# First-phase attention heads straight from PSUM behind the key units, and one 512-token range for group 0's output projection and first norm

## The chip, the cores and the metric

The kernel runs on one core of one Trainium2 chip. The metric is device time in microseconds, from one launch, and lower is better. In the tables, PE is TensorE (matmuls), PEld its weight loads, DVE VectorE, ACT ScalarE, POOL GpSimd, and SP the SyncE engine, whose queue issues nearly all DMA.

## The reference

One layer of a hybrid encoder runs over two groups of tokens with the same weights: 1024 tokens of a new stream ("prompt") and 32 tokens of a running stream with a cache of 256 ("sample"). All arithmetic is float32.

```python
mod = silu(c) @ w_ada + b_ada                       # six vectors of 1024 per stream
h = x * (1 + sc1) + sh1
mq, mk, mv, mo, mi, mf, fq, fk, fv, ff, gu, gv = split(h @ w_in)
hm = head_norm(mlstm(mq, mk/8, mv, mi, mf)) * g * sigmoid(mo)   # 4 heads of 64, chunked recurrence
hf = softmax(fq fk^T / 8 + F_t - F_s, causal) @ fv              # 8 heads of 64, F = cumsum(log_sigmoid(ff))
hg = gu * (tril(ws) @ layer_norm(gv) + bs)                      # 4 groups, blocks of 128 tokens
mix = concat(hm, hf, hg) @ w_o
x = layer_norm(ALPHA * x + (1 + g1) * mix)
y = (silu(h2 @ w_gate) * (h2 @ w_up)) @ w_down      # h2 = x * (1 + sc2) + sh2, width 2816
x = layer_norm(ALPHA * x + (1 + g2) * y)
```

The outputs are x and the states: the attention's keys, values and log forget values, and the mLSTM's matrices.

## The kernel before

**Layout and precision.** Activations lie transposed, features on the 128 partitions and tokens along the free axis, in 8 tiles of 128 features. The 1056 tokens are cut into group 0 (tokens 0 to 511) and group 1 (512 to 1055, the sample in its last 32). A float32 product is made from three passes in TensorE's fast float32 type: each operand is split into a high part and a remainder, and `gemm` (L111) adds hi x hi, hi x lo and lo x hi, at lines L117, L118 and L119. `weights` (L94) loads 512 KB into one of three "raw" buffers (L87 is the load in `load`), makes the high part on ScalarE (L105) and the remainder on VectorE or POOL (L106). A matmul writes into a PSUM bank of 512 columns; the pool "g" has three.

**Ranges.** `MM` cuts each group into two ranges, (0, 256) and (256, 512) for group 0 and two of 272 for group 1. `WIDE` is the single range (0, 512).

**Order.** The code is traced in program order. The Tile framework then fixes each engine's instruction order ahead of the run, from priorities (program order) and its own model of the timing. `tc.high_priority(n)` moves the traced instructions up by n places and `issue_after` puts them behind a given one. On the chip every engine runs its list strictly in order, SP's DMA list included.

**Stages around the change.** After the first units come the values and gates (`gates`: the cumulative sums and maxima of the forget values, long chains on VectorE over few partitions, that store the rows `dfs` which every attention head reads). Then follows the string `ORDER`, unit by unit: `q`h makes queries and keys of attention head h, `f`h attends for the head's first 512 queries, `k0 k1` make the mLSTM's keys (`k1p`: its weights' remainder on POOL), `s` prepares the mLSTM's states, `m`j is its chunk j, `v` and `o` are units with tokens on the partitions, `a` is one unit of `ada` (two loads of 512 KB, 16 matmuls, two transposes, a ScalarE copy and four small VectorE operations). `f` and `m` run at high priority.

A `q` unit before the change is `fm_unit` with `evac_qk` for each range: ScalarE makes the high part `qkh` (L366), VectorE the remainder `qkl` (L367), POOL their sum `qkr` (L368) for the key output; all three are stored (`dqh`, `dql`, `o_kT`). `fox` (L672) then loads nine pieces back into the tiles k1, k2, qp, q2 and v. The scores are L717 and L718, the softmax's exponential L726, the transposes L753, the products with the values L761 and L766.

After the phase come the gMLP units, the second-half tokens of heads 2 and 3, and group 0's output projection: `wo` is called once for each range of 256, so it loads the eight weight tiles of w_o twice. Each output tile passes `sublayer_end`: POOL subtracts the pivot (`less`, L977), VectorE adds the residual (L982), and `ln_sum` squares on ScalarE (L871) and adds up on POOL (L875) and VectorE (L877). `ln1` then takes the means through TensorE (L887), the reciprocal root (L894 to L898), and per tile a multiplication (L999), an addition (L1000), an affine on ScalarE (L1003) and the split into `hh` (L1007) and `hl` (L1008), the operands of the up projection. The four units of heads 4 to 7 for group 1's tokens follow, then `ln1_res` (the residual's affine, 16 operations on POOL, L1017), the second phase's attention and the feed-forward units `up` (SiLU at L1055 to L1059) and `down`. The ada units 20 to 23 come behind the first four up units.

Of the kernel before, what the change touches and what calls it, by code (L numbers as in the profile page):

```python
# [7 lines left out]
F32 = mybir.dt.float32  # L8
F32R = mybir.dt.float32r
# [6 lines left out]
P = 128  # L16
D = 1024
KT = 8
# [23 lines left out]
ORDER = "q0 f0 q1 a f1 a q2 f2 k0 k1p s a q3 f3 a v q4 f4 a q5 f5 o a m0 q6 f6 a m1 q7 m2 f7 a m3"  # L42
# [23 lines left out]
def f(ap):  # L66
    return ap.bitcast(F32)


class Kernel:  # L70
# [288 lines left out]
    def evac_qk(self, h):  # L359
        nc = self.nc  # L360

        def evac(o, n, ps):
            hi = self.t(self.sm, [P, 272], F32R, "qkh", 3)
            lo = self.t(self.sm, [P, 272], F32R, "qkl", 2)
            kr = self.t(self.sm, [P, 272], F32, "qkr", 3)
# [9 lines left out]

    def evac_mqk(self, i, scale):
        nc = self.nc

        def evac(o, n, ps):
            r = self.t(self.sm, [P, 272], F32, "qkr", 3)  # L380
# [291 lines left out]
    def fox(self, h, chunks):  # L672
# [4 lines left out]
        t = lambda shape, dt, tag, bufs: self.t(mx, shape, dt, tag, bufs)  # L677
        b = self.foxbufs
        k1 = t([P, nk], F32R, "k1", b[0])
        qp = t([P, nq], F32R, "qp", b[1])  # L680
        k2 = t([68, nk], F32R, "k2", b[2])
        q2 = t([68, nq], F32R, "q2", b[1])
        v = t([P, nb, P], F32R, "v", b[3])
        qs = slice(q0, q1)
        self.load(f(qp[0:64]), self.dqh[h, 0:64, qs])
        self.load(f(qp[64:128]), self.dql[h, 0:64, qs])
        self.load(f(k1[0:64]), self.dqh[h, 64:128, :nk])
        self.load(f(k1[64:128]), self.dqh[h, 64:128, :nk])
        self.load(f(q2[0:64]), self.dqh[h, 0:64, qs])
        self.load(f(q2[64:68]), self.dfs[h, 2:6, qs])  # L690
        self.load(f(k2[0:64]), self.dql[h, 64:128, :nk])
        self.load(f(k2[64:68]), self.dfs[h, 0:4, :nk])
        self.load(f(v), self.dv[:, :nb, h * P:(h + 1) * P])
# [5 lines left out]
    def fox_chunk(self, h, tiles, W, nq, k1, k2, qp, q2, v):  # L699
# [71 lines left out]
        tmp = t([64, nq], F32, "fo", 1)  # L771
        r = t([64, nq], F32, "fr", 1)
        nc.scalar.copy(tmp[:, :nq], o[64:128, :nq])
        nc.vector.tensor_tensor(r[:, :nq], o[0:64, :nq], tmp[:, :nq], ALU.add)
# [80 lines left out]

    def ln_pivot(self, st, z, sl):
# [7 lines left out]
    def ln_sum(self, st, z, m, sl):  # L864
# [5 lines left out]
        sq = self.t(self.p2, [P, 272], F32, "tmp", 4)[:, :sl.stop - sl.start]  # L870
# [29 lines left out]
    def ln_stats(self, st, sl):  # L900
# [3 lines left out]
        v = self.t(self.p2, [P, 272], F32, "tmp", 4)[:, :sl.stop - sl.start]  # L904
# [68 lines left out]
    def sublayer_end(self, c, z, m, ps, gate, st, a, b):  # L973
# [3 lines left out]
        less = lambda: self.nc.gpsimd.tensor_tensor(z[:, m, sl], z[:, m, sl], st["pv"][:, sl], ALU.subtract)  # L977
# [13 lines left out]
    def ln1(self, c, st, a, b):  # L991
# [3 lines left out]
        for k in range(KT):  # L995
# [4 lines left out]
            (nc.gpsimd if k % 4 == 1 else nc.vector).tensor_tensor(zk, zk, e, ALU.add)  # L1000
            h = self.t(self.p2, [P, 272], F32, "tmp", 4)[:, :b - a]
# [250 lines left out]
    def run(self):  # L1252
# [71 lines left out]
        self.foxbufs = (2, 1, 1, 2, 3)  # L1324

        def emit(x):
# [7 lines left out]
            if x[0] == "q":  # L1334
                self.fm_unit(w3[2 + i], self.evac_qk(i), (0, 1) if i < QD else (0,), eng)
# [63 lines left out]
        for g, (j0, nj) in enumerate(GROUPS):  # L1399
# [195 lines left out]
```

## Time and profile before

| | us |
|---|---|
| median of 3 runs | 1391.1 (1388.4 to 1398.72) |
| profiled execution | 1389.64 |
| its span, first to last instruction | 1387.8 |
| PE busy | 1344.1 (97%) |
| DVE busy | 1030.4 (74%) |
| ACT busy | 641.0 (46%) |
| POOL busy | 260.2 (19%) |

The mean granted TensorE clock is 0.990 of full speed. A row of a view of groups reads: line, engine, operation, tile written <- tiles read, shapes, count | busy us, mean ns of one | idle us of the engine just before them and what ended it. A row of waits reads: the waiting instruction <- what released it: us in total, times, longest. A row of the chain or of the timeline begins with its start in us.

### The profile page before, as it was taken

How to read it: one execution, taken by the hardware profiler on the slowest of the kernel's cores; microseconds unless marked ns; L12 is line 12 of the kernel's file. 1: busy time of each engine (PE TensorE's matmuls, PEld its weight loads, DVE VectorE, ACT ScalarE, POOL GpSimd, SP SyncE). 2: the span in 40 equal slices, each digit the busy share in tenths (PEclk: the TensorE clock that was granted, in tenths of full speed). 3: DMA queues.
4: the chain of work that ended last, by engine and by line, in shares of the span. 5: the costliest groups of instructions: out<-in, count | busy, mean ns of one | idle time of the engine just before them, and what ended most of it. 6: DMA issues, size and time to landing. Idle time of an engine off the chain costs nothing.

```text
span 1387.8 us, 25846 instructions
## 1 busy us (share of the span) xinstructions
PE 1344.1 (97%) x9651; PEld 1236.2 (89%) x9651; DVE 1030.4 (74%) x2190; ACT 641.0 (46%) x1249; POOL 260.2 (19%) x292
## 2 busy tenths in 40 slices
PE   7999999999999799999999999999999999999996
PEld 4899988899999678888887889899999999999996
DVE  5548656678788657777776766678898988888777
ACT  3313234444555344545544455345574544545355
POOL 0103200052267400000000000264610000000341
PEclk9999999999999899999999999999999999999998
DMA  9764577585765665554543442564587767453321
GB/s 361 260 217 135 165 239 213 173 252 167 234 209 152 194 182 155 141 140 118 138 117 86 112 122 81 192 176 132 159 221 200 217 163 205 145 176 113 102 90 65
DMA packets 133557, 233.09 MB, mean 168 GB/s; under 512 B 22308, under 2 KB 75180, under 8 KB 133432
## 3 DMA queue, kind: packets, MB, share of 16 engines
q1 hardware_dynamic: 128120, 221.34, 51.7%
q0 software_dynamic: 5168, 9.96, 4.7%
q8 instruction: 76, 1.25, 0.4%
q14 instruction: 49, 0.40, 0.1%
q10 hardware_dynamic: 144, 0.14, 0.0%
HBM read 197.50 MB, written 53.81 MB: 181 GB/s over the span
## 4 chain that ended last, share of the span: by engine, by line
PE 69%; DVE 4%; DMA 2%; ACT 1%; issue 1%; POOL 0%; SPq 0%; DVEq 0%; ACTq 0%
PE up_g L117 5%; PE up_g L118 5%; PE up_g L119 5%; PE dn_g L119 4%; PE dn_g L117 4%; PE dn_g L118 4%; PE sup_u L119 3%; PE sup_u L117 3%; PE sup_u L118 3%; PE wo_g L118 2%; PE wo_g L119 2%; PE wo_g L117 2%; PE sup_g L118 2%; PE sup_g L119 2%; PE sup_g L117 2%; PE fox_t L753 2%
## 5 line engine op out<-in xcount | busy, mean ns | idle before, releaser
L117 PE MATMUL up_g<-mlstm_ah,up_whi 128*128 128x512 f32 (+1 forms) x384 | 142.8, 372 | 3.6 <-DVE fm_qkl L367 2.7
L118 PE MATMUL up_g<-mlstm_al,up_whi 128*128 128x512 f32 (+1 forms) x384 | 143.0, 372 | 0.6 <-DVE mlstm_al L1008 0.6
L119 PE MATMUL up_g<-mlstm_ah,up_wlo 128*128 128x512 f32 (+1 forms) x384 | 142.4, 371 | 0.0
L284 PE MATMUL tm_g<-tm_whi,start_h1l 128*128 128x256 f32 (+1 forms) x384 | 110.0, 287 | 0.0
L282 PE MATMUL tm_g<-tm_whi,start_h1h 128*128 128x256 f32 (+1 forms) x384 | 109.6, 287 | 0.0
L283 PE MATMUL tm_g<-tm_wlo,start_h1h 128*128 128x256 f32 (+1 forms) x384 | 109.5, 286 | 0.0
L117 PE MATMUL fm_g<-start_h1h,fm_whi 128*128 128x256 f32 (+2 forms) x344 | 102.1, 302 | 6.9 <-DVE fm_qkl L367 2.7
L118 PE MATMUL fm_g<-start_h1l,fm_whi 128*128 128x256 f32 (+2 forms) x344 | 101.5, 295 | 0.2 <-DVE start_h1l L223 0.2
L119 PE MATMUL fm_g<-start_h1h,fm_wlo 128*128 128x256 f32 (+2 forms) x344 | 100.6, 294 | 0.0
L1127 ACT CAST sup_whi<-sup_raw 128x1024 fp32r<-128x1024 f32 x54 | 56.0, 1048 | 90.3 <-PE dn_u L118 46.5
L117 PEld LDWEIGHTS up_g<-mlstm_ah,up_whi 128*128 128x128 f32 x384 | 74.5, 194 | 16.2 <-DVE fm_qkl L367 2.9
L118 PEld LDWEIGHTS up_g<-mlstm_al,up_whi 128*128 128x128 f32 x384 | 74.6, 194 | 12.6 <-DVE up_actl L1061 0.8
L119 PEld LDWEIGHTS up_g<-mlstm_ah,up_wlo 128*128 128x128 f32 x384 | 74.6, 194 | 10.7
L105 ACT CAST up_whi<-up_raw 128x1024 fp32r<-128x1024 f32 x50 | 52.4, 1049 | 61.1 <-PE dn_g L118 22.5
L726 ACT ACTIVATE fox_p<-fox_s,fox_fmx 128x384 f32<-128x384 f32 (+2 forms) x96 | 55.1, 579 | 49.1 <-DVE fox_fmx L724 43.6
L117 PEld LDWEIGHTS fm_g<-start_h1h,fm_whi 128*128 128x128 f32 x344 | 65.3, 191 | 12.7 <-DVE fm_qkl L367 3.2
L982 DVE SCALAR_TENSOR_TENSOR wo_z<-dn_g,start_mod,wo_z 128x512 f32<-128x512 f32 (+4 forms) x120 | 60.3, 521 | 21.1 <-PE dn_g L119 20.5
L1128 DVE TENSOR_TENSOR sup_wlo<-sup_raw,sup_whi 128x1024 fp32r<-128x1024 f32 x54 | 68.0, 1263 | 10.4 <-ACT sup_whi L1127 10.4
L282 PEld LDWEIGHTS tm_g<-tm_whi,start_h1h 128*128 128x128 f32 x384 | 72.3, 189 | 1.9 <-issue 1.2
L284 PEld LDWEIGHTS tm_g<-tm_whi,start_h1l 128*128 128x128 f32 x384 | 72.3, 188 | 1.5 <-issue 1.2
L117 PE MATMUL dn_g<-up_acth,dn_whi 128*128 128x512 f32 (+2 forms) x200 | 73.5, 368 | 0.0
L118 PE MATMUL dn_g<-up_actl,dn_whi 128*128 128x512 f32 (+2 forms) x200 | 73.4, 368 | 0.0
(571 smaller groups left out, 4591.4 us busy)
## 6 DMA issues: line engine op xcount, KB each, us to landing
up_raw<-w_gu SPq DMA_DIRECT2D x50, 512.0 KB
dn_raw<-w_dn SPq DMA_DIRECT2D x28, 512.0 KB
ada_late<-w_ada SPq DMA_DIRECT2D x24, 512.0 KB
wo_raw<-w_o SPq DMA_DIRECT2D x24, 512.0 KB
sup_raw<-w_gu SPq DMA_DIRECT2D x20, 512.0 KB
start_dp<-w_gu SPq DMA_DIRECT2D x19, 512.0 KB
start_dp<-w_gu POOLq DMA_DIRECT2D x19, 512.0 KB, 7.7
sup_raw<-start_dp SPq DMA_DIRECT2D x18, 512.0 KB
```

The costliest lines, as they stand in the source:

```text
L105: nc.scalar.copy(hi[:, :w], raw[:, :w])
L117: nc.tensor.matmul(ps, hi, xh(k), start=start and k == 0, stop=False)
L118: nc.tensor.matmul(ps, hi, xl(k), start=False, stop=False)
L119: nc.tensor.matmul(ps, lo, xh(k), start=False, stop=stop and k == n - 1)
L282: nc.tensor.matmul(ps[:, :ncol], xh, hi, start=k == 0, stop=False)
L283: nc.tensor.matmul(ps[:, :ncol], xh, lo, start=False, stop=False)
L284: nc.tensor.matmul(ps[:, :ncol], xl, hi, start=False, stop=k == 7)
L726: nc.scalar.activation(pr[:, lo:hi], banks[x][:, :hi - lo], AF.Exp, bias=mxs[:, 0:1], accum_out=sums[:, x:x + 1])
L753: nc.tensor.transpose(ps[:, c:c + P], probs[y][:, b * P:(b + 1) * P], self.ident)
L982: self.lastz = self.nc.vector.scalar_tensor_tensor(z[:, m, x:y], ps[:, x - a:y - a], g[i], z[:, m, x:y], ALU.mult, ALU.add)
L1127: nc.scalar.copy(h, x)
L1128: tt(l, x, f(h), ALU.subtract)
```

## The change

1. **Heads from PSUM.** The new `head_unit` makes the first 512 tokens of a head in one range of 512 columns and writes the attention's tiles k1, k2, qp and q2 directly from the PSUM bank, by four ScalarE copies and two VectorE subtractions; two more ScalarE copies feed the key output. Only the keys' parts are stored for the second phase. The gates' rows and the values are loaded ahead of the unit's matmuls. The tiles' buffers go from (2, 1, 1, 2) to (2, 2, 2, 2), and the evacuation's `qkh` and `qkr` from 3 to 2.
2. **Order.** The mLSTM's key units `k0 k1p` move ahead of all heads, and the ada entries shift with them.
3. **Group 0's projection and norm.** `wo` and `ln1` run once over the range of 512; the pivot subtraction, the running sum and the additions that were POOL's go to VectorE for group 0. A pool of wide temporaries is opened for the stretch. The evacuations of heads 4 to 7 behind it run at high priority, each followed by one of the ada units 20 to 23.
4. **First up unit.** Unit 0 of `up` runs over 512 columns too.

```diff
-ORDER = "q0 f0 q1 a f1 a q2 f2 k0 k1p s a q3 f3 a v q4 f4 a q5 f5 o a m0 q6 f6 a m1 q7 m2 f7 a m3"
+ORDER = "k0 k1p q0 f0 q1 a f1 s a q2 f2 a q3 f3 a v q4 f4 a q5 f5 o a m0 q6 f6 a m1 q7 m2 f7 a m3"
...
+    def head_unit(self, h):
+        nc = self.nc
+        w = self.weights(self.d["w_in_f"][2 + h], KT, P)
+        self.phase = "head"
+        k1, k2, qp, q2, v = self.heads[h] = self.head_tiles(h, 512, 512)
+        self.load(f(q2[64:68]), self.dfs[h, 2:6, :512])
+        self.load(f(k2[64:68]), self.dfs[h, 0:4, :512])
+        self.load(f(v), self.dv[:, :4, h * P:(h + 1) * P])
+        ps = self.t(self.pg, [P, 512], F32, "g")
+        self.gemm(ps, w, slice(0, P), *self.h1parts(0, 512))
+        lo, hi = slice(0, 64), slice(64, 128)
+        nc.scalar.activation(qp[lo], ps[lo], AF.Copy, scale=0.125)
+        nc.vector.scalar_tensor_tensor(qp[hi], ps[lo], 0.125, f(qp[lo]), ALU.mult, ALU.subtract)
+        nc.scalar.copy(k1[hi], ps[hi])
+        nc.vector.tensor_tensor(k2[lo], ps[hi], f(k1[hi]), ALU.subtract)
+        nc.scalar.copy(k1[lo], ps[hi])
+        nc.scalar.activation(q2[lo], ps[lo], AF.Copy, scale=0.125)
+        for o in (0, 256):
+            kr = self.t(self.sm, [P, 272], F32, "qkr", 2)
+            nc.scalar.copy(kr[hi, :256], ps[hi, o:o + 256])
+            self.store(self.d["o_kT"][h, :, o:o + 256], kr[hi, :256])
+        self.store(self.dqh[h, hi, :512], f(k1[hi]))
+        self.store(self.dql[h, hi, :512], f(k2[lo]))
+        if h < QD:
...
+    def late(self, evac):
+        def first(o, n, ps):
+            with self.tc.high_priority(HPA):
+                evac(o, n, ps)
+        return first
...
-        less = lambda: self.nc.gpsimd.tensor_tensor(z[:, m, sl], z[:, m, sl], st["pv"][:, sl], ALU.subtract)
+        less = lambda: (self.nc.gpsimd if c else st["eng"]).tensor_tensor(z[:, m, sl], z[:, m, sl], st["pv"][:, sl],
+                                                                          ALU.subtract)
...
-            (nc.gpsimd if k % 4 == 1 else nc.vector).tensor_tensor(zk, zk, e, ALU.add)
-            h = self.t(self.p2, [P, 272], F32, "tmp", 4)[:, :b - a]
+            (nc.gpsimd if c and k % 4 == 1 else nc.vector).tensor_tensor(zk, zk, e, ALU.add)
+            h = self.ltmp(b - a)
...
-        self.foxbufs = (2, 1, 1, 2, 3)
+        self.foxbufs = (2, 2, 2, 2, 3)
...
-                self.fm_unit(w3[2 + i], self.evac_qk(i), (0, 1) if i < QD else (0,), eng)
+                self.head_unit(i)
...
-        st = self.ln_begin(nc.gpsimd)
-        for cut in MM[0]:
-            self.wo(0, st, (cut,), nc.vector)
-        self.operand(0, self.ph)
-        for a, b in MM[0]:
-            weave(self.ln1(0, st, a, b))
+        sw = ExitStack()
+        self.pw = self.pool("pw", ctx=sw)
+        st = self.ln_begin(nc.vector)
+        self.wo(0, st, WIDE, nc.vector)
+        weave(self.ln1(0, st, *WIDE[0]))
         for h in range(PRE, 8):
-            self.fm_unit(w3[2 + h], self.evac_qk(h), (1,))
+            self.fm_unit(w3[2 + h], self.late(self.evac_qk(h)), (1,))
+            self.ada(16 + h, self.wp, "raw", RAW, self.pg, "g")
+        sw.close()
         self.ln1_res(0)
...
-                weave(self.up(0, j, act, pa, WIDE if 0 < j < GROUPS[-1][0] else MM[0]))
-                if j < 4:
-                    self.ada(20 + j, self.wp, "raw", RAW, self.pg, "g")
+                weave(self.up(0, j, act, pa, WIDE if j < GROUPS[-1][0] else MM[0]))
```

More of the change, by code (lines that the diff above doesn't have):

```diff
@@ L770, in fox_chunk @@
             nc.tensor.matmul(o[:, :nq], v[:, 0, :], held[:, :nq], start=False, stop=True)
[L771 to L774, printed above, removed]
+        r = t([64, nq], F32, "fo", 1)
+        nc.scalar.copy(r[:, :nq], o[64:128, :nq])
+        nc.vector.tensor_tensor(r[:, :nq], o[0:64, :nq], r[:, :nq], ALU.add)
         c = tiles[0] // 4
@@ L1323, in run @@
         self.mx = self.pool("mx0", ctx=s2)
-        self.foxbufs = (2, 1, 1, 2, 3)
+        self.foxbufs = (2, 2, 2, 2, 3)
+        self.heads = {}
         def emit(x):
```

56 lines of the change are left out of this document (34 added, 22 removed).

## The prediction

> **What bounds the kernel now.** I read the page first, then busy time by stage, then the list of what TensorE waited for, then the chain of waits around its longest gaps.
>
> ```profile
> span 1387.8 us, 25846 instructions
> PE 1344.1 (97%) x9651; PEld 1236.2 (89%) x9651; DVE 1030.4 (74%) x2190; ACT 641.0 (46%) x1249; POOL 260.2 (19%) x292
> ```
>
> TensorE is busy for 97%. No other engine is near, so an edit pays only where it shortens TensorE's own work or closes a gap in it. The change acts on four stages, here as windows (columns: stretch, length, busy time and instructions of PE, PEld, DVE, ACT and POOL, granted clock, DMA share, GB/s): gates with the first units, the phase of the first eight attention chunks, group 0's output projection, and the norm with the four units behind it.
>
> ```profile
> 105.00:168.00 63.00, 60.30 (x496) 59.36 (x495) 47.89 (x115) 17.74 (x39) 19.45 (x29) 0.97 0.48 142
> 168.00:379.00 211.00, 204.59 (x1689) 189.34 (x1688) 142.47 (x411) 95.03 (x229) 39.07 (x46) 1.00 0.71 213
> 379.00:427.00 48.00, 48.00 (x396) 47.59 (x397) 41.61 (x52) 24.07 (x36) 33.91 (x30) 1.00 0.69 211
> 427.00:480.00 53.00, 45.05 (x316) 42.32 (x315) 38.84 (x84) 25.39 (x58) 29.07 (x36) 0.87 0.58 159
> ```
>
> TensorE idles 2.70 us in the first window, 6.41 in the second, nothing in the third, 7.95 in the fourth. The clock column tells of a second loss there (0.97, 0.87), cut finer here:
>
> ```profile
> 138.30:141.00 2.70, 0.02 (x1) 0.00 (x0) 2.64 (x4) 0.00 (x0) 0.95 (x2) 0.96 0.21 63
> 141.00:144.20 3.20, 3.18 (x15) 3.18 (x16) 3.07 (x6) 2.01 (x4) 2.20 (x3) 0.50 0.40 129
> 452.80:455.50 2.70, 0.04 (x1) 0.00 (x0) 0.55 (x2) 0.00 (x0) 0.00 (x0) 0.87 0.46 128
> 455.50:461.60 6.10, 6.10 (x28) 6.10 (x29) 6.03 (x13) 1.44 (x2) 3.76 (x5) 0.50 0.62 194
> 464.10:465.80 1.70, 0.50 (x3) 0.27 (x2) 1.70 (x6) 1.70 (x6) 1.70 (x2) 1.00 0.19 22
> 469.40:473.40 4.00, 0.00 (x1) 0.01 (x1) 2.89 (x6) 0.24 (x2) 2.14 (x5) 0.81 0.82 215
> 473.40:478.70 5.30, 5.30 (x32) 4.03 (x33) 2.55 (x10) 0.75 (x2) 0.00 (x0) 0.50 1.13 227
> ```
>
> Behind each long gap the clock stands at 0.50, which throws away half of the following busy time: 1.6, 3.05 and 2.65 us. So the gap at 138 costs 2.7 + 1.6 = **4.3**, and the norm's stretch 2.7 + 3.05 + 1.2 + 4.0 + 2.65 = **13.6**. The Trainium skill (TensorE: Matmul & The Clock Gate, the table of the two states) puts the half clock behind an idle window of about 3.4 us. The trace shows it behind 2.70 us, so the measurement decides; by the page's figure such a gap would cost 2.7 rather than 4.3.
>
> What TensorE waited for (total, times, longest), and the chain through the norm (start, us):
>
> ```profile
> PE fox_s L717 <- DMA fox_qp<-start_dql: 4.3, 3, 1.7
> PE ada_g L179 <- DVE up_sil L1059: 4.1, 1, 4.1
> PE fm_g L117 <- DVE fm_qkl L367: 2.7, 1, 2.7
> PE up_g L117 <- DVE fm_qkl L367: 2.7, 1, 2.7
> ```
>
> ```profile
> 448.50 6.33 DMA start_dql<-fm_qkl
> ...
> 464.59 2.56 POOL wo_z L1017 x2
> 467.14 0.75 POOL fm_qkr L368
> 467.91 1.96 DMA o_kT<-fm_qkr
> ...
> 473.40 1.93 PE ada_g L179 x16
> ```
>
> At 455 a key evacuation on VectorE waits for its buffer's store, and TensorE for the bank that it frees. At 464 to 473 the residual's affine on POOL (L1017) holds up the key sum (L368) and its store; VectorE waits for it, then a SiLU, then TensorE.
>
> **The change, part by part.**
>
> *Wider matmuls.* Rates of 256, 512 (two rows, fifteen steps apart) and 272 columns:
>
> ```profile
> 386.30:409.00 22.70, 22.70 (x193) 1.00 0.67 208
> 561.51 0.39 PE L118 MATMUL up_g<-mlstm_al,up_whi 128*128 128x512 f32 x1
> ...
> 565.01 0.39 PE L118 MATMUL up_g<-mlstm_al,up_whi 128*128 128x512 f32 x1
> 440.00:452.00 12.00, 11.96 (x95) 1.00 0.58 163
> ```
>
> A 256-column matmul takes 22.70/193 = 0.1176 us, a 512 one 3.50/15 = 0.2333: 0.002 less than two halves. Pairs: 192 in the projection, 8 x 24 in the heads, 48 in the first up unit, 432 in all: **-0.8 us**. The halved instruction count buys nothing else on TensorE, which is already saturated at 256.
>
> *Heads straight from PSUM.* The durations for this and the norm:
>
> ```profile
> L366 ACT ACTIVATE fm_qkh<-fm_g,start_qsc 128x256 fp32r<-128x256 f32 x16 | 7.6, 473 | 8.7 <-PE fm_g L119 7.9 <-issue 0.7
> L758 ACT CAST fox_pth<-fox_t 128x512 fp32r<-128x512 f32 x48 | 27.6, 587 | 25.0 <-PE fox_t L753 25.0
> L1059 DVE TENSOR_TENSOR up_sil<-up_g,up_sil 128x512 f32<-128x512 f32 x17 | 11.7, 688 | 6.1 <-PE up_g L119 6.0
> L367 DVE SCALAR_TENSOR_TENSOR fm_qkl<-fm_g,start_qsc,fm_qkh 128x272 fp32r<-128x272 f32 x16 | 7.9, 494 | 8.9 <-DMA start_dql<-fm_qkl 6.7 <-POOL fm_qkr L368 1.1 <-ACT up_whi L105 1.1
> L106 DVE TENSOR_TENSOR fm_wlo<-fm_raw,fm_whi 128x1024 fp32r<-128x1024 f32 x17 | 21.3, 1260 | 8.7 <-ACT fm_whi L105 8.6
> L982 DVE SCALAR_TENSOR_TENSOR wo_z<-dn_g,start_mod,wo_z 128x512 f32<-128x512 f32 x40 | 29.9, 747 | 15.6 <-PE dn_g L119 15.2
> L877 DVE TENSOR_TENSOR wo_qs<-wo_qs,wo_tmp 128x256 f32<-128x256 f32 x14 | 12.1, 862 | 0.0
> L877 DVE TENSOR_TENSOR up_qs<-up_qs,dn_tmp 128x256 f32<-128x256 f32 x14 | 6.1, 475 | 2.5 <-ACT dn_tmp L871 2.4
> L999 DVE TENSOR_TENSOR wo_z<-wo_z,wo_pv 128x256 f32<-128x256 f32 x16 | 7.8, 557 | 0.0
> L1017 POOL TENSOR_SCALAR wo_z<-wo_z,start_colp 128x256 f32<-128x256 f32 x16 | 17.2, 1082 | 2.7 <-ACT lna_tmp L1003 2.7
> ```
>
> Before, a head's first 512 tokens cost ScalarE 2 x 0.473; after, four copies of 512 at 0.587 and two of 256 at about 0.47 make 3.3. That is 2.4 more for each of eight heads, 19 us on an engine 45% busy in that stage: no cost while it stays ahead of a unit of 24 x 0.2333 = 5.6 us, and 2.4 a head if it does not. VectorE pays 2 x 0.69 instead of 2 x 0.48. POOL loses the sums. Six loads and two half stores of a head go; those of k1 and k2 for the second phase stay. The query operand then no longer arrives by DMA, so the 4.3 us of waits have no cause. What is left by DMA, the rows 64:68 and the values, is issued ahead of the unit's matmuls. Bounds: all of it gone, or all of it kept because the rows of the gates come late instead. I take 1.3 kept: **-3.0**.
>
> *Key units first.* Their evacuation is one ScalarE copy, so TensorE's banks no longer depend on VectorE, which is in the gates' chain (47.89 busy of 63). That takes the cause of the 2.7 gap away. But the first head now comes behind 2 x 48 matmuls of key units and still needs the gates' rows stored and loaded back; if VectorE is as late as now, the scores wait in the projection's place. Bounds 0 and 4.3; half: **-2.2**.
>
> *Projection and norm in one range.* The weights of the projection are loaded, cast and split 8 times, not 16: 8 x 1.26 us of VectorE and 4 MB less. The pivot subtraction and the running sum move from POOL to VectorE, at 0.69 each. Per output tile VectorE then does 1.26 + 0.75 + 3 x 0.69 = 4.1 against 5.6 on TensorE: hidden. What matters is the end. From the last projection matmul, the statistics take VectorE and ScalarE some eleven 512-wide steps in series and two matmuls, about 8 us. Then come 8 x 3 wide operations at 0.69 (16.5), eight key evacuations at 0.49 (4.0), four weight splits (5.0) and the four moved ada units' small operations (3, an estimate): 36.5 us. TensorE's filler is 8 x 24 x 0.1263 = 24.2, four ada units at 1 us of matmuls each (1.93 at half clock) and about 0.4 for their transposes, and the means: 31.5. The first up unit reads tile k at 31.5 + 0.7 k, the last one at 36.4. It is **just enough**, where before the second half's norm began with the filler nearly over. Before, half-range 2 had nothing behind it but up units that needed it.
>
> The moved ada units also bring 8 loads of 512 KB past the key units' loads and stores in SP's queue. Filler loads and stores come to 4 x 1.5 + 2.7 = 8.9 MB and up's weights 1 MB; with 1.5 MB prefetched, 8.4 MB in 31.5 us need 267 GB/s. The stages above ran 211 to 213. At that rate the data take 39.5 us, 8 more than the filler. So the residue of the 13.6 lies between 0 and 8 + 3 (one half-clock stretch). The buffers of the evacuation fall from 3 to 2; the low part already had 2, and it was the one waited for at 455, so I count nothing. Since L999 (0.557) shows some slowing beside POOL, I take 4.2: **-9.4**.
>
> *Sum*: -0.8 - 3.0 - 2.2 - 9.4 = -15.4 from the profiled execution's own 1389.6 (span 1387.8 and 1.8 around it; the median shown is 1391.1, 0.1% above): **1374**.
>
> **Rivals.**
>
> *The filler runs out.* VectorE's 24 wide operations run beside POOL's 16 affines (17 us). L877 beside a busy POOL took 0.862, beside an idler one 0.475, a factor of 1.81. With it the list grows by 13.4 to 49.9; TensorE waits 13.5 and loses 3 to the clock: 16.5 in place of 13.6. 1389.6 + 2.9 - 6.0 = **1387**. For it: nothing moved POOL's affines away. Against: L999 saw the same neighbour and took only 0.557. The Trainium skill (SBUF — State Buffer, the shared port pair as an exclusive lock) says that such a VectorE operation is blocked for the whole of POOL's instruction; 16 blocks of 1.08 would add 17 us instead of 13.4 and give 1390, and the two L877 rows fit it better than L999 does.
>
> *The first phase keeps its waits*, moved from the query's load to the gates' rows: 1389.6 - 9.4 - 0.8 = **1379**. For it: VectorE's gates chain is untouched and long. Against: the key units cover 96 x 0.12 more.
>
> *Slower: SP's queue blocks.* A head's loads now stand in front of its unit, and two buffers mean that head h's wait for the last read of head h-2. Everything behind in SP's queue, weights above all, waits too.
>
> ```profile
> SPq L87 <- PE fox_o L766: 21.3, 6, 8.5
> ```
>
> SP has waited up to 8.5 us on exactly such a matmul. For six heads, 8.5 less the 5.6 of one unit in hand is 2.9 idle, and 1.7 for the clock: 27.6. 1389.6 - 10.2 + 27.6 = **1407**. It decides once the wait outlasts the weights that three raw buffers hold. Against: the value and gate units between heads hold TensorE for 8 x 24 x 0.1176 = 22.6 us each, and a head gives its buffers back in that time.
>
> *That nothing changes* (the order was already set by other waits) would give 1390; the named releasers speak against it.
>
> **How the numbers follow.** Forecast 0.52, filler out 0.19, first phase kept 0.17, SP 0.10, nothing 0.02. The forecast's own range is 1367 (every term at its best: 0.8 + 4.3 + 4.3 + 13.6 = 23.0 off) to 1381 (residue 11). To leave no more than two tenths out, the range runs to **1363** (an order that also closes waits outside these stages) and **1393**. Faster by over 1%, under 1377.2, which is about what a measurement of this kernel can tell from no change: four fifths of the forecast, a third of the kept first phase and a little of the rest, 0.52. Slower by over 1%, above 1405: 0.09. Within: 0.39.
>
> **What would show it.** Right: no wait of fox_s for fox_qp's load; no half clock near 140; TensorE busy over 50 of the 53 us behind the projection; group 0's L877 and L862 without POOL beside them. Wrong step by step: scores waiting for the rows 64:68 (gates late); up's first matmuls waiting for L1008 (filler short) or ada for its load (DMA); SP waiting long on fox_o with weight casts behind it. If TensorE idles as much as before, 1387.8 - 1344.1 = 43.7 us, the forecast has failed.

## The result

The changed kernel takes 1393.8 us (median of 20 runs, 1390.4 to 1397.4), the kernel before 1390.1 (20 runs on the same chip). The ratio is **1.0023, 95% interval 1.0012 to 1.0034**: about 3.2 us slower, where 15.4 us less were forecast. Ratios below are against runs of the kernel before on the same chip in the same session, since its own median went from 1386.3 to 1392.3 between sessions; us are worked out at 1390.

The page of the changed kernel, and three of the four windows shown before (stretch, length, busy time and instructions of PE, PEld, DVE, ACT, POOL, granted clock, DMA share, GB/s); in the one left out, 379 to 427, TensorE is busy throughout, as it was:

```profile
span 1389.4 us, 24723 instructions
PE 1343.9 (97%) x9213; PEld 1216.4 (88%) x9213; DVE 1018.5 (73%) x2152; ACT 641.7 (46%) x1241; POOL 212.6 (15%) x244
105.00:168.00 63.00, 59.72 (x429) 54.67 (x428) 45.22 (x126) 21.29 (x48) 12.77 (x20) 0.95 0.41 122
168.00:379.00 211.00, 205.84 (x1547) 186.09 (x1546) 146.28 (x405) 106.68 (x253) 32.39 (x37) 0.98 0.59 182
427.00:480.00 53.00, 44.43 (x300) 37.70 (x299) 33.60 (x60) 22.04 (x37) 27.28 (x31) 0.87 0.56 176
```

The work that was to go did go: 438 fewer matmuls (the 432 counted, and 6 products of the statistics), 48 us less of POOL, 12 of VectorE. TensorE idles 45.5 us (1389.4 - 1343.9) where it idled 43.7. In the last window it idles 8.57 us where it idled 7.95, at the same clock. The waits that hold it are other ones than before (us in total, times, longest; only the row of fm_qkl was there, with one wait of 2.7 at 138):

```profile
PE fm_g L117 <- DVE fm_qkl L367: 6.5, 3, 4.2
PE mlstm_t L605 <- DVE fox_ptl L801: 2.8, 1, 2.8
PE ada_t L179 <- DMA ada_late<-w_ada: 2.7, 1, 2.7
PE wo_g L117 <- ACT up_ah L987: 2.0, 2, 1.8
PE ada_g L179 <- DVE ada_adam L187: 1.9, 1, 1.9
```

The scores' wait for fox_qp is gone, as forecast. In its place stand a modulation unit that waits for its load (at 157), an mLSTM transpose (at 307, the releaser named is VectorE's list), a modulation unit among the late query and key units (ada_g, at 443), these units themselves (L367, 4.2 of it at 457), and, 400 us further on, group 1's output projection (wo_g, near 900). Windows of three of the gaps, each with the stretch behind it:

```profile
156.70:159.40 2.70, 0.03 (x1) 0.00 (x0) 2.09 (x6) 2.21 (x6) 0.00 (x0) 0.92 0.95 264
159.40:165.80 6.40, 6.33 (x31) 5.55 (x32) 2.56 (x9) 2.80 (x8) 1.70 (x3) 0.50 0.72 225
306.80:309.50 2.70, 0.00 (x1) 0.00 (x0) 2.70 (x13) 1.54 (x4) 0.50 (x2) 0.94 0.28 81
309.50:312.60 3.10, 3.03 (x14) 2.85 (x14) 2.49 (x9) 1.06 (x3) 1.08 (x2) 0.51 0.99 217
457.10:461.30 4.20, 0.01 (x3) 0.00 (x1) 2.69 (x4) 4.20 (x8) 4.20 (x7) 0.77 0.14 41
461.30:466.20 4.90, 4.90 (x21) 4.90 (x22) 2.58 (x4) 2.45 (x6) 4.90 (x7) 0.50 0.78 250
```

### The profile page after: what moved, and what is told of

It is laid out like the page before. It is cut to its first block, busy times and chain, and to the rows that moved or that the text cites. A ratio compares the mean times of both kernels' runs of the same rounds, so it can differ in the third digit from the quotient of the medians.

```text
span 1389.4 us, 24723 instructions
## 1 busy us (share of the span) xinstructions
PE 1343.9 (97%) x9213; PEld 1216.4 (88%) x9213; DVE 1018.5 (73%) x2152; ACT 641.7 (46%) x1241; POOL 212.6 (15%) x244
## 4 chain that ended last, share of the span: by engine, by line
PE 82%; DVE 7%; DMA 5%; issue 2%; ACT 1%; POOL 1%; SPq 0%; DVEq 0%; POOLq 0%; ACTq 0%
PE up_g L119 6%; PE up_g L117 6%; PE up_g L118 6%; PE dn_g L119 4%; PE dn_g L117 4%; PE dn_g L118 4%; PE tm_g L283 3%; PE tm_g L282 3%; PE tm_g L284 3%; PE sup_u L119 3%; PE sup_u L117 3%; PE sup_u L118 3%; PE fox_t L795 2%; PE wo_g L118 2%; PE wo_g L119 2%
## 5 line engine op out<-in xcount | busy, mean ns | idle before, releaser
L117 PE MATMUL up_g<-mlstm_ah,up_whi 128*128 128x512 f32 (+1 forms) x368 | 137.7, 374 | 1.5 <-ACT up_whi L105 1.5
L119 PE MATMUL up_g<-mlstm_ah,up_wlo 128*128 128x512 f32 (+1 forms) x368 | 137.7, 374 | 0.2 <-DVE up_wlo L106 0.2
L118 PE MATMUL up_g<-mlstm_al,up_whi 128*128 128x512 f32 (+1 forms) x368 | 137.3, 373 | 0.0
L117 PEld LDWEIGHTS up_g<-mlstm_ah,up_whi 128*128 128x128 f32 x368 | 69.2, 188 | 13.9 <-ACT up_whi L105 2.0
L119 PEld LDWEIGHTS up_g<-mlstm_ah,up_wlo 128*128 128x128 f32 x368 | 69.2, 188 | 12.4 <-DVE up_wlo L106 0.4
L118 PEld LDWEIGHTS up_g<-mlstm_al,up_whi 128*128 128x128 f32 x368 | 69.3, 188 | 11.7
L283 PEld LDWEIGHTS tm_g<-tm_wlo,start_h1h 128*128 128x128 f32 x384 | 72.5, 189 | 2.3 <-issue 2.1
L105 ACT CAST up_whi<-up_raw 128x1024 fp32r<-128x1024 f32 x50 | 52.3, 1047 | 46.8 <-PE up_g L118 23.4
L106 DVE TENSOR_TENSOR up_wlo<-up_raw,up_whi 128x1024 fp32r<-128x1024 f32 x50 | 62.6, 1251 | 15.5 <-ACT up_whi L105 14.8
L119 PE MATMUL dn_g<-up_acth,dn_wlo 128*128 128x512 f32 (+2 forms) x200 | 73.2, 366 | 0.0
L800 ACT CAST fox_pth<-fox_t 128x512 fp32r<-128x512 f32 (+1 forms) x80 | 41.2, 543 | 67.4 <-PE fox_t L795 67.3
```

The lines of the kernel that those rows point to most:

```text
L105: nc.scalar.copy(hi[:, :w], raw[:, :w])
L106: (eng or nc.vector).tensor_tensor(lo[:, :w], raw[:, :w], f(hi[:, :w]), ALU.subtract)
L117: nc.tensor.matmul(ps, hi, xh(k), start=start and k == 0, stop=False)
L118: nc.tensor.matmul(ps, hi, xl(k), start=False, stop=False)
L119: nc.tensor.matmul(ps, lo, xh(k), start=False, stop=stop and k == n - 1)
L283: nc.tensor.matmul(ps[:, :ncol], xh, lo, start=False, stop=False)
```

## The experiments

**First reading.** From the trace alone I held that the key sum on POOL was the cause of the stop at 457: it took 4.70 us at 445 where it takes 0.76 at 456, then stood behind six of the residual's scalings, and SyncE's queue waited in order for its store with the next weights' load behind (timelines of POOL and SyncE, start and length in us):

```profile
445.21 4.70 POOL L368 TENSOR_TENSOR fm_qkr<-fm_qkh,fm_qkl 128x272 f32<-128x272 f32 x1 [6.76 <-DVE fm_qkl L367]
449.89 6.81 POOL L1064 TENSOR_SCALAR wo_z<-wo_z,start_colp 128x256 f32<-128x256 f32 x6
456.66 0.76 POOL L368 TENSOR_TENSOR fm_qkr<-fm_qkh,fm_qkl 128x272 f32<-128x272 f32 x1
449.94 0.47 SPq L91 DMA_DIRECT2D o_kT<-fm_qkr  x1
451.13 0.40 SPq L87 DMA_DIRECT2D fm_raw<-w_in_f  x1
```

Four kernels: each half of the change alone, and two that take this suspect away.

```diff
 first_only: ORDER, head_unit, buffers as changed;
-  wo/ln1 over WIDE, late(), ada behind the late units, up 0 over WIDE
+  wo/ln1 over MM[0], evac_qk, ada behind the first four up units, up 0 over MM[0]
 norm_only: the reverse (three buffers for the evacuation's qkh and qkr, as before)
 key_sum_act, in evac_qk of the late units:
-  nc.gpsimd.tensor_tensor(kr[:, :n], f(hi[:, :n]), f(lo[:, :n]), ALU.add)
+  nc.scalar.activation(kr[:, :n], ps, AF.Copy, scale=self.qsc)
   ... (the copy of the sample's keys out of kr goes from POOL to ScalarE as well)
 affine_last:
-  self.ln1_res(0)
+  with tc.issue_after(self.lastq.ins):   # the last key sum's copy on POOL
+      self.ln1_res(0)
```

> This kernel has the changed first phase (key units first, heads from PSUM) and the old projection, norm, first range of up and places of the modulation. Theory one (the first phase lost and the norm stretch gave nothing): three TensorE gaps near 157, 307 and 368 us, 2.75 + 2.76 + 1.97 us with half clock behind each, come again, and the time is about 4 us above before: 1393 to 1395 us. Rival (the first phase gained its 5 us as forecast, and the wide norm lost 8 to 9): 1384 to 1386 us. Second rival (what moved is only how later work falls, by chance): anywhere within 3 us of before, without the three gaps.

Measured: **0.9974 (0.9959 to 0.9989)**, 3.6 us faster than before. The rival came nearest (1384 to 1386 on a chip where before took 1390.5; 1386.5 measured). Yet the three gaps of theory one are there too:

```profile
PE ada_t L179 <- DMA ada_late<-w_ada: 2.6, 1, 2.6
PE fm_g L117 <- DVE fm_qkl L367: 2.5, 2, 2.1
PE mlstm_t L605 <- DVE fox_ptl L801: 2.4, 1, 2.4
```

```profile
105.00:168.00 63.00, 59.66 (x429) 54.60 (x428) 45.50 (x126) 21.29 (x48) 12.84 (x20) 0.95 0.40 122
168.00:379.00 211.00, 205.12 (x1546) 184.76 (x1545) 145.92 (x405) 106.44 (x253) 32.66 (x37) 0.99 0.59 183
427.00:480.00 53.00, 46.69 (x347) 44.03 (x347) 42.98 (x91) 27.28 (x61) 31.74 (x37) 0.97 0.61 166
```

Up to 379 it idles 3.34 + 5.88 = 9.2 us (before 9.1) and loses more to the clock (0.95 and 0.99 where it was 0.97 and 1.00). By the traces the gain lies in the norm stretch, whose code is that of before but for the evacuation's two buffers: idle 6.3 for 7.95, clock 0.97 for 0.87, which is 1.6 + 0.10 x 53 = 6.9 us by this fixed window. So a change in the phase ahead would have moved how the next stage's waits fall. That is read from one trace of each kernel, taken in different sessions, and not shown: order_before, below, has the same norm stretch in its trace (6.51 of idle, clock 0.97) and no gain in time.

> This kernel has the changed projection, norm, first range of up and places of the modulation, and the first phase of before (old order, heads through memory, three buffers each for the high halves and the key sums). Theory one (the first phase lost about 4 us, the norm stretch is even): 1389 to 1391 us, with TensorE idle near 443 and 457 us as in the changed kernel. Rival (the wide norm lost what the first phase gained): 1397 to 1400 us. Third theory (the gaps of the norm stretch come of two buffers for high halves and key sums where there were three): with three again the gaps near 443 and 457 us are gone, about 9 us with the half clock, and the time is 1380 to 1383 us.

Measured: 1.0019 (1.0008 to 1.0031), 2.6 us slower. The three buffers' theory missed the time by some 9 us, and the gap near 446 stayed (1.95 us). But the one near 459 did not stay as it was. It is 1.7 us, where it was 4.2, and it waits for ScalarE's cast of the weights:

```profile
PE fm_g L117 <- ACT fm_whi L105: 1.7, 1, 1.7
```

With three buffers ScalarE made the high part (L366) ahead of that cast, at 454.27, and not behind it. The norm stretch keeps 7.24 of idle at clock 0.94, which is 5 us less than in the changed kernel by the same working (7.24 + 0.06 x 53 = 10.4 against 15.5, in a trace of its slowest run, 1395.8). The two halves do not add up (-3.6 + 2.6 is not +3.2), and the 4.2 us between is near to that. Whether the third buffer would give it back in the changed kernel, no run shows.

> The changed kernel, with one thing other: in the units behind the wide norm the key sum is no GpSimd addition of the two halves but a ScalarE copy of the bank (0.125 or 1 times), so that neither VectorE's norm nor GpSimd's six residual scalings stand ahead of the key store in SyncE's queue. Theory one (the key sum on GpSimd, 4.70 us instead of 0.76 beside the norm and then 6.81 us behind the scalings, holds the queue and with it the loads of the next weights): the gap of 4.19 us near 457 us and its half clock of 6.9 us go, and with them part of the 2.7 us near 443; 1384 to 1388 us. Rival one (VectorE's norm is too long for the filler, whoever sums the keys): the gaps stay, since the evacuation L367 on VectorE is what TensorE waits for; 1392 to 1395 us. Rival two (the moved modulation loads crowd the memory path): unchanged, 1392 to 1395 us.

> The changed kernel, with the residual scalings of ln1_res(0) on GpSimd put behind the last key sum of the late units. Theory one: the second key sum, which waited 6.81 us behind six scalings, comes up to 6 us sooner, the next weights with it, and the gap of 4.19 us near 457 us shrinks to under 1 us with no half clock behind it, while the first key sum still takes 4.70 us beside the norm: 1387 to 1390 us. Rival one (VectorE's norm itself): 1392 to 1395 us. If the scalings are then late for the residual of the next stage, a new wait of TensorE on them shows behind 500 us and the gain is less.

Measured: 1.0033 (1.0014 to 1.0051) and 1.0060 (1.0038 to 1.0082): **theory one missed both times**, neither is faster than the changed kernel, and the first has the time that its rivals gave. The gap at 457 stays, 3.7 and 4.2 us, in the second with the same releaser (L367), in the first with another:

```profile
PE fm_g L117 <- ACT fm_qkr L369: 3.7, 1, 3.7
```

With the sum on ScalarE the weights were loaded 2.7 us earlier, and then the evacuation itself stood behind three of the norm's affines (L1056) and a split in ScalarE's list:

```profile
455.12 1.53 ACT L1056 ACTIVATE lna_wide<-wo_z,wo_lnb,wo_lng 128x512 f32<-128x512 f32 x2
...
457.77 0.47 ACT L366 ACTIVATE fm_qkh<-fm_g,start_qsc 128x272 fp32r<-128x272 f32 x1
```

The new copy reads the bank too. It came at 460.25 (L369), behind more of the norm, while VectorE had read the bank by 458.78. So this kernel put a wait of its own in the old one's place, and does not clear the key sum. affine_last could not move the load: it was issued at 451.13, behind the first key store alone, and the scalings stood ahead of the second (457.45).

What held TensorE can be read in the changed kernel's own lists. ScalarE's and then VectorE's rows for the stop at 457, and VectorE's for the one at 443:

```profile
456.79 1.04 ACT L105 CAST fm_whi<-fm_raw 128x1024 fp32r<-128x1024 f32 x1 [5.75 <-DMA fm_raw<-w_in_f]
457.74 1.51 ACT L1050 ACTIVATE lna_wide<-wo_z,wo_lnb,wo_lng 128x512 f32<-128x512 f32 x2
459.67 0.48 ACT L366 ACTIVATE fm_qkh<-fm_g,start_qsc 128x272 fp32r<-128x272 f32 x1
457.86 1.24 DVE L106 TENSOR_TENSOR fm_wlo<-fm_raw,fm_whi 128x1024 fp32r<-128x1024 f32 x1 [2.53 <-ACT fm_whi L105]
```

```profile
439.75 4.89 DVE L1046 TENSOR_TENSOR wo_z<-wo_z,wo_pv 128x512 f32<-128x512 f32 x8
444.56 0.17 DVE L187 TENSOR_REDUCE ada_adam<-ada_g 128x4 f32<-128x16 f32 x1
```

At 443 a modulation unit's small reduction (L187) waits behind eight wide multiplications on VectorE. At 457 VectorE is not the engine that is short of time: it idled 2.53 us for ScalarE's weight cast (L105). ScalarE had idled 5.75 us for the weights, whose load stood in SyncE's queue behind the store of the slow key sum; then the evacuation's high part (L366) stood behind that cast and the norm's affines. Ahead of the stop VectorE is full. The same 21 us (436 to 457) of before and of the changed kernel:

```profile
436.00:457.00 21.00, 18.30 (x138) 17.83 (x137) 14.52 (x30) 11.49 (x26) 15.33 (x17) 0.95 0.51 145
436.00:457.00 21.00, 18.25 (x140) 15.69 (x132) 19.21 (x35) 8.22 (x15) 13.55 (x10) 0.84 0.55 173
```

VectorE is busy 19.21 of 21 us against 14.52, but within the stop itself 2.69 of 4.20, where ScalarE and POOL have 4.20 (the window at 457 above). So several lists fall due at one place, the key sum's among them, and no run takes one of them away cleanly.

**Second theory: the attention slides.** All four kernels so far with the wide norm and the moved modulation, and neither of the two without, idle 3 to 4 us near 900. In these, the last attention chunk of the second phase ends late. ScalarE's last copy of that phase (L773 before, L814 after), with the first matmul of group 1's projection; before, then the changed kernel:

```profile
874.33 0.37 ACT L773 COPY fox_fo<-fox_o 64x256 f32<-64x256 f32 x1 [2.44 <-PE fox_o L766]
901.01 0.29 PE L117 MATMUL wo_g<-up_ah,wo_whi 128*128 128x272 f32 x1
```

```profile
886.61 0.37 ACT L814 COPY fox_fo<-fox_o 64x256 f32<-64x256 f32 x1 [1.80 <-PE fox_o L808]
897.03 0.29 PE L117 MATMUL wo_g<-up_ah,wo_whi 128*128 128x272 f32 x1
```

The result goes through memory and a split to be the projection's operand. It had 26.7 us for that, and has 10.4. The instruction order is fixed ahead of the run by the framework's model of the timing. As I read the code, the attention starts in it when the late units free their memory, so that whatever stretches these moves all sixteen chunks among the MLP's matmuls; no run shows that step by itself. Counted in the order of TensorE's instructions, the last chunk stands behind 53.4 MLP units of 24 matmuls before and behind 56.3 after (in the traces 76 matmuls more, which is 3.2 units).

```diff
 ada_behind (from the changed kernel): the four self.ada(16 + h, ...) behind the loop over h, not in it
 ada_moved_only (from before): the four ada between the late units, nothing else
 heads_only (from first_only): ORDER of before
 order_before (from before): ORDER of the change
```

> The changed kernel with the four modulation units that now stand between the late query and key units put behind the last of these. Theory two (new): the modulation units stretch the late units, whose end frees the memory of the second phase's attention; its chunks then fall later among the MLP's matmuls, so that the last attention chunk ended 12.3 us later than before (887.0 instead of 874.7 us) and the operand of group 1's projection, which goes through memory, comes late: 3.3 us of TensorE idle between 900 and 912. In this kernel the last chunk stands behind as many MLP matmuls as before (53.4 instead of 56.3 units of 24 of them). So the idle at 900 to 912 is gone, up_pv is made near 875 and not 888, and the time is 1386 to 1390 us. Rival one (VectorE's norm is too long, wherever the modulation stands): gaps of the norm stretch and time stay, 1392 to 1395. Rival two (group 1's operand is late because GpSimd's pivot subtractions slow VectorE's split, 0.85 us instead of 0.44, whenever they come): the idle at 900 stays even with the attention early.

Measured: 1.0066 (1.0043 to 1.0088). The idle near 900 is gone (80.00 busy of 80 us from 880 to 960), but the kernel is 9 us slower than before, where theory two had it level or faster: four modulation units in a row wait for their loads (3.8 us) and copies (3.3 us). The norm stretch:

```profile
427.00:480.00 53.00, 42.41 (x284) 32.32 (x283) 36.37 (x70) 20.07 (x35) 24.34 (x31) 0.77 0.59 167
```

> The kernel before, with one thing of the change alone: the four modulation units that stood behind the first MLP units stand between the late query and key units. Projection and norm stay in two ranges, the first phase stays as it was. Theory two (attention slides against the MLP): the last attention chunk comes 2.3 MLP units of 24 matmuls later (55.7 instead of 53.4), about 12 us, and group 1's projection waits some 3 us near 900; against it the wait of the modulation for the SiLU at 469 (4.05 us and 2.65 of half clock) can go at best: between 1386 and 1394 us with the idle at 900 in the trace. Rival (the slide costs nothing, the wide norm alone brings the idle at 900): no idle there, and 1383 to 1388.

Measured: 1.0027 (1.0011 to 1.0042), 3.7 us slower, with the old norm. The idle near 900 came without the wide norm:

```profile
PE wo_g L117 <- ACT up_ah L941: 3.6, 1, 3.6
```

> Of the change only the heads from PSUM: the old order of the first phase (query units first), old projection and norm. The prediction's term for this was 3.0 us less: the three waits of the scores for the query load (4.3 us) go, 1.3 kept. Theory one: the gap at 138 (2.7 us and half clock) stays or goes, since the wide unit's evacuation is six copies on ScalarE and two on VectorE; the gaps near 157 and 307 of the whole first phase are not there, since they come of the order; 1385 to 1388 us. Rival (heads cost what they save, the gain of 3.9 us of the whole first phase is the order's): 1389 to 1391.

Measured: 1.0195 (1.0174 to 1.0217), 27 us slower: missed by both theories. TensorE runs out of work at 131, before the gates are ready:

```profile
PE gates_t L537 <- DVE gates_rs L532: 23.6, 1, 23.6
```

> The kernel before with only the order of the first phase changed: the key units of the mLSTM first, heads still through memory. The prediction's term for this was 2.2 us less. Theory one: the gap at 138 goes, the wait of the modulation for its load near 157 comes in its place, and the waits for the query load stay: 1389 to 1392 us. Rival (the order alone brings the first phase's gain): 1385 to 1388.

Measured: 1.0004 (0.9990 to 1.0018). The order alone does nothing that could be told; heads without it cost 27 us; together they save 3.6. Their terms can't be had apart.

**The norm stretch taken apart, and two tries at the first phase.**

```diff
 ada_back (from the changed kernel): ada 20 to 23 behind up 0 to 3 again; up 0 stays over WIDE
 ada_back_split (from ada_back): up 0 over MM[0] again
 first_a_later (from first_only):
-  ORDER "k0 k1p q0 f0 q1 a f1 s a q2 ..."
+  ORDER "k0 k1p q0 f0 q1 f1 a s a q2 ..."
 first_geng (from first_only):
-  GENG = (0, 1, 1, 0)
+  GENG = (0, 0, 0, 0)      # weight remainders of four late units: none on POOL
```

> The changed kernel with the four modulation units again behind the first four MLP units; projection, norm and first MLP unit stay in ranges of 512. Theory two (what costs is how late the second phase's attention falls among the MLP's matmuls): the last chunk stands behind 55.7 units of 24 matmuls here, against 56.3 in the changed kernel and 53.4 before, so the idle of 3 to 4 us near 900 stays, while the 4.2 us and half clock near 457 change to a wait of the modulation for the SiLU: 1389 to 1393 us. Rival (the moved modulation itself, by its loads in SyncE's queue and its small operations on VectorE, was the whole loss): 1383 to 1386.

> As the kernel with the modulation behind the MLP units, but the first MLP unit in two ranges of 256 again: of the norm stretch only the projection and the norm in one range of 512 are left, and the first phase of the change. The last attention chunk stands behind 53.4 units, as before. Theory two: no idle near 900, up_pv near 873; 1383 to 1387 us, which is the time of the first phase alone (3.6 us below before) give or take 2, since the wide norm alone neither wins nor loses. The prediction's own term for the wide norm (9.4 less) would give 1377. Rival (VectorE's wide norm loses by itself what the filler can't cover): 1389 to 1393, with 8 us or more of idle between 427 and 480.

Measured: 1.0038 (1.0020 to 1.0056) and 1.0005 (0.9986 to 1.0023). In the first the idle near 900 is there, as theory two had it. In the second theory two missed: near 900 there is no idle, as it said, but the time is level with before and not 3 to 7 us under it; the rival, that the wide norm loses by itself, has both the time and the idle of 8 us or more. In us against before, four kernels that differ by one step each: first phase -3.6; with projection and norm in one range (and the late evacuations at high priority) +0.7; with the first up unit in one range too +5.3; with the modulation moved (the change) +3.2. The steps are **-3.6, +4.3 (1.0 to 7.6), +4.6 (1.0 to 8.2) and -2.1 (-5.0 to 0.8)**. The third step changes where the attention falls (53.4 to 55.7 units), and the idle near 900 with it; the norm stretch of ada_back_split, then 880 to 960 of ada_back (80.00 of 80 busy in ada_back_split):

```profile
427.00:480.00 53.00, 44.15 (x294) 40.61 (x294) 38.29 (x61) 24.75 (x41) 27.31 (x31) 0.91 0.53 145
```

```profile
880.00:960.00 80.00, 77.06 (x556) 74.22 (x555) 55.48 (x79) 29.23 (x57) 40.22 (x37) 0.96 0.62 174
```

2.9 us of idle and 0.04 x 80 = 3.2 of clock. And the wide projection and norm by themselves: idle 8.85 and clock 0.91 in the norm stretch, against 6.31 and 0.97 with two ranges, which is 2.5 + 3.2 = 5.7 for the 4.3 measured. There too an evacuation waits on the key sum, here for the buffer that the sum reads (ScalarE's row in ada_back_split; the sum on POOL took 4.18 us):

```profile
456.38 0.49 ACT L366 ACTIVATE fm_qkh<-fm_g,start_qsc 128x272 fp32r<-128x272 f32 x1 [4.80 <-POOL fm_qkr L368]
```

> The changed first phase with old projection and norm, and one modulation unit of the first phase one place later in the order: behind the second head's attention instead of ahead of it. Theory: its load is issued behind the first head's stores in SyncE's queue and TensorE waited 2.6 us for it at 157, with 6.8 us of half clock behind; one place later the load has landed, the gap and its clock go: 3 to 6 us less than with the first phase alone, 1381 to 1384 us beside 1386.5 there. Rival (another unit's wait, the first scores for the gates' rows or their operand split, takes its place): within 1.5 us of the first phase alone.

Measured: 0.9966 (0.9949 to 0.9984), the same as the first phase alone within 1.5 us, as the rival had it. The gap stays at 157 (3.0 us), so the unit's place in the string was not its cause.

> The changed first phase with old projection and norm, and all four late value units' weight remainders on VectorE instead of two of them on GpSimd. Theory: the gap of 2.4 us near 307 comes of four VectorE operations (L592) that took 5.3 us instead of 1.4 while GpSimd made two remainders of 2.4 us; without these on GpSimd the gap goes: 1 to 3 us less than the first phase alone (1386.5). Rival: VectorE pays eight remainders of 1.26 us more between 300 and 380, where it was busy 32 of 40 us, and the evacuation at 368 comes later still: 1386 to 1390.

Measured: 0.9953 (0.9931 to 0.9975); against the first phase alone 0.9979, with an interval (0.9952 to 1.0006) that holds no change. The mechanism is there: VectorE's four mLSTM operations beside POOL's remainders, and without them (first_only, then first_geng):

```profile
L592 DVE SCALAR_TENSOR_TENSOR mlstm_mw<-mlstm_mb,start_col,start_maskbig 128x128 f32<-128x128 f32 x4 | 5.3, 1384 | 0.0
```

```profile
L592 DVE SCALAR_TENSOR_TENSOR mlstm_mw<-mlstm_mb,start_col,start_maskbig 128x128 f32<-128x128 f32 x4 | 1.1, 339 | 0.0
```

**The slide without the rest.** Two kernels from first_geng: fg_late adds the late evacuations' high priority; fg_act adds to that the key sums on ScalarE. They have the old norm, and modulation and up as before. before_geng is before with GENG all zero.

> The changed first phase, old projection and norm, all weight remainders of the late value units on VectorE (these three together took 0.47% off the kernel before), and in addition the evacuations of the late query and key units at high priority, as the change has them. The last attention chunk stands behind 53.4 MLP units, as before. Theory two: no idle near 900; 0.4 to 0.7% below before. If the high priority helps (the waits for fm_qkl at 451 and for the norm at 458), up to 3 us less than without it.

> As the kernel beside it, with one thing other: the key sums of the late units are ScalarE copies of the bank in place of GpSimd additions. The work of the MLP, the norm and the modulation is the same, and the modulation stands where it stood; but the last attention chunk falls behind 55.7 MLP units in place of 53.4. Theory two (how late the attention falls is what costs): TensorE idles 3 us or more between 895 and 910 with half clock behind, up_pv comes 10 us or more later, and the time is 3 to 5 us above the kernel beside it. Rival (the idle at 900 belongs to the wide norm or to the moved modulation): no idle there, and within 1.5 us of the kernel beside it or less.

Measured: 0.9928 (0.9907 to 0.9950) and **0.9918 (0.9888 to 0.9948)**. The idle near 900 follows the attention's place once more (the norm stretch of fg_late, which is busy for all of 880 to 960; then both windows of fg_act), yet the time does not show it: the ratio of the two is 0.9990 (0.9952 to 1.0027), where 3 to 5 us more were expected. In the two-range norm the key sum on ScalarE gives back as much:

```profile
427.00:480.00 53.00, 46.97 (x331) 43.40 (x330) 40.87 (x92) 28.01 (x63) 29.08 (x37) 0.94 0.61 169
```

```profile
427.00:480.00 53.00, 49.54 (x356) 45.34 (x355) 42.05 (x95) 34.88 (x81) 21.64 (x25) 1.00 0.66 190
880.00:960.00 80.00, 76.99 (x618) 76.45 (x617) 62.45 (x103) 36.06 (x74) 44.43 (x42) 1.00 0.62 177
```

Near 900 it loses 3.0 us, in the norm stretch it gains 2.6 of idle and 0.06 x 53 = 3.2 of clock.

> The kernel before with one thing other: all weight remainders of the late value units on VectorE. Theory (the gain came of the changed first phase's gap at 307, which GpSimd's remainders caused): here there was no such gap, so within 1.5 us of before. Rival (the remainders on GpSimd cost in any order): 2 to 4 us below before.

Measured: 1.0062 (1.0035 to 1.0089), 8.6 us slower: in its trace group 0's projection, which waited for nothing before, idles 5.5 us from 379 to 427, 3.0 of them for VectorE's evacuation L367. Both expectations missed: the same edit costs here, and costs nothing that could be told behind the changed first phase. fg_act, 0.8% under before, is the best version found.

## Why the prediction was wrong

**The failing step** is the term of 9.4 for projection and norm, in the sentence that takes 4.2 as the residue of the 13.6. In the window used there (427 to 480, with the clock's share taken over all of it) the changed kernel keeps 8.57 of idle and 0.13 x 53 = 6.9 of clock, 15.5; before it was 7.95 and the same 6.9. The wide projection and norm by themselves cost 4.3, and the two edits with them 2.5.

- *The count of 36.5 us of VectorE against 31.5 of filler* was near in its parts: the three wide operations of a tile took 0.68, 0.70 and 0.77 on the mean, hardly slowed by POOL, so the rival of the slowed norm has nearly the right size (16.5) by the wrong mechanism. What failed was to hold the filler to be independent. Each filler unit needs an evacuation, a weight split and small operations from VectorE and ScalarE, and these stand in the same lists as the wide norm. TensorE did not run dry behind the filler; it stopped inside it, at 443 (1.9 us) and 457 (4.2). At 443 VectorE's list is what it waited for. At 457 it was SyncE's queue and ScalarE's list: the weights came late, behind the store of a key sum that took 4.70 us, and the evacuation stood behind their cast and the norm's affines. The count had neither the queue's order nor ScalarE in it. It had the loads as bytes, 8 us at the most; but 134 GB/s moved from 445 to 451, while the queue stood, and 212 from 451 to 457, when the late weights came, so traffic can be a part of that wait and not its start. Which of these lists would have to go first, no run shows.
- *Two buffers for three* was put at nothing, because the low part was the one waited for. In norm_only, with three, the wait at that place is 1.7 us and not 4.2, and in ada_back_split, with two, the high part waited 4.80 us for a buffer. What that is worth in time was not measured.
- *The moved modulation* was costed by its matmuls, small operations and loads in the stretch itself. That it and the wide first up unit would move sixteen attention chunks 400 us later was not in the sum. It shows as 2.9 to 4.1 us of idle near 900 in every kernel with the last chunk at 55.7 units or later, with both norms, and in none at 53.4.
- *Heads from PSUM (-3.0) and key units first (-2.2)*: the sum of 5.2 against 3.6 (1.5 to 5.7) measured looks right and is not. The waits named did go (fox_qp; the half clock near 140), but gaps at 157 and 307 took their place, the one at 368 grew (1.4 to 2.1 in first_only), and the phase itself gained nothing by its windows; by the traces the gain stands in the norm stretch behind it. As far as the traces tell, that the sum came near is luck. The rival *first phase keeps its waits* had that much right, though by other waits than the gates' rows. To halve the term for the order and cost the heads by themselves was wrong: either without the other gives nothing or a loss of 27 us.
- *Wider matmuls*: -0.8 is below what these runs can tell.
- *The filler's bytes*: 4 x 1.5 + 2.7 is 8.7 MB and not 8.9; the bound of 8 us falls by less than 1, and nothing that failed hangs on it.
- *SyncE's queue blocks*: it now waits for the last scores of a head that hold the tiles, not for the values, and at most 2.7 us, under the 5.6 us of one unit in hand, so the price did not come (queue waits of the changed kernel, 100 to 380):

```profile
SPq L87 <- PE fox_s L760: 5.7, 4, 2.7
```
- *What would show it wrong* held: TensorE idle still at 45.5 us.

What stays open: where the first phase's 3.6 us come from, what the third buffer is worth beside the wide norm, and which order of the wide norm and the late evacuations would let the wide norm win. None of these was tried.

## What to carry to other kernels

Filler is only filler if its evacuations do not queue on the engines that it is meant to cover: cost the two as one list per engine, in order, with the load queue as one of the engines. Where a framework fixes the order from a modelled time, an edit in one stage moves instructions hundreds of us away; compare the order of the busiest engine, and the slack between a producer and its consumer (here 26.7 us against 10.4), before trusting a local sum. And parts of a change are to be measured in steps on top of each other, not alone: two first-phase edits were worth +0 and +27 us apart and -3.6 together.

## What was not expected of the hardware

A POOL addition of 128x272 took 4.70 us instead of 0.76 while VectorE ran, back to back, operations such as these:

```profile
445.05 1.88 DVE L1047 TENSOR_TENSOR wo_z<-wo_z,wo_qs 128x512 f32<-128x512 f32 x3
446.85 1.21 DVE L106 TENSOR_TENSOR fm_wlo<-fm_raw,fm_whi 128x1024 fp32r<-128x1024 f32 x1
```

In the other direction, L592 on VectorE took 1.38 us instead of 0.34 beside POOL's remainders. The Trainium skill (SBUF — State Buffer, on the shared port pair) says that the loser blocks for the whole of the other's instruction. The trace agrees in kind; but the addition lost 3.9 us, more than any one of VectorE's operations beside it took (0.5 to 1.2), so it seems to have waited for several in a row. Every kernel with the wide norm that leaves these sums on POOL has one of 2.9 to 4.7 us in this stretch; in the others none took over 1.73. And the clock fell to 0.50 behind the gaps of 2.7 us at 157 and 307 of the changed kernel, and even behind the one of 1.9 at 443 (0.50 from 445.7 to 452.5), though not behind the one of 2.4 at 307 in first_only (2.50 us with 0.08 busy, then full speed):

```profile
307.50:310.00 2.50, 0.08 (x1) 0.00 (x0) 2.50 (x12) 1.54 (x4) 0.49 (x1) 1.00 0.28 80
310.00:313.40 3.40, 3.39 (x28) 3.32 (x29) 2.78 (x11) 1.40 (x4) 1.03 (x2) 1.00 0.99 240
```
